# A two-layer diffusion trunk: K and V projected by stream, a hand-given order in the first FFN unit, and the output stored in four parts

## The chip, the cores and the metric

The kernel runs on one core of a Trainium2 chip. The metric is the device time of one launch in microseconds (us), the median of three runs. Five engines work side by side, each with its own instruction queue that it takes strictly in order: PE (TensorE, matrix products; its weight loads are listed as PEld), DVE (VectorE), ACT (ScalarE), POOL (GpSimd) and SP (SyncE, which issues most DMAs). They wait for one another through semaphores. Data come from the chip's main memory by DMA into on-chip memory; PE writes its results into eight accumulator banks (PSUM), of which this kernel gives four to running products (tag `acc`) and four to everything short-lived (tag `aux`).

## The reference, cut to what matters

Two streams of 256 tokens each, the latent `x` (v = 0) and the context `ctx` (v = 1), width D = 1024, go through two layers. Everything is in 32-bit floats.

```
for i in range(2):
    m, mc = split9(silu(c) @ w_ada[i] + b_ada[i]), split9(silu(c_ctx) @ w_ada[i] + b_ada[i])
    x  += 0.5*m[2]  * swiglu(rms(x,  g0)*(1+m[1])  + m[0])          # and xc the same way with mc
    h, hc = rms(x, g1)*(1+m[4]) + m[3], rms(xc, g1)*(1+mc[4]) + mc[3]
    k, v of both streams (two attention branches); q, conv, gates of the latent stream
                                                   (and, in layer 0, of the context as well)
    x  += m[5] * merge(window attention, gated conv, global attention)
    x  += 0.5*m[8] * swiglu(rms(x, g2)*(1+m[7]) + m[6])
return x                                            # latent stream only, (1, 256, 1024)
```

`w_ada[i]` is 1024 x 9216: shift (column block 0) and scale (block 1) of the first norm are needed before the first product of the layer. `swiglu(h) = (silu(h @ wg) * (h @ wu)) @ wd` with an inner width of 2816. The input projection's first 512 columns are K and V of branch a (128 each) and of branch c (128 each).

## The kernel before, in words

**Layout.** Activations are kept transposed, channels on the 128 partitions: `xT` is 128 x 8 x 512 (eight blocks k of 128 channels; columns 0 to 255 are the latent tokens, 256 to 511 the context). Each product is made three times to keep 32-bit accuracy: an operand is split into a high and a low part (`wh`, `wl` for weights; `hh`, `hl` for activations), and PE adds wh·hh, wh·hl and wl·hh (lines 207 to 209, or 1088 to 1090 in the first unit). Splitting 128 x 1024 weights takes a copy on ACT (line 184 or 191) and then a subtraction on DVE (line 185 or 192). The tags `wh` and `wl` have three buffers. One 128-column block of weights against all tokens is 24 products (8 blocks k times 3) into one `acc` bank, 512 columns wide, or 256 wide for one stream alone.

**Order.** The program is written in one thread. A planner then gives each engine its order: an instruction that it thinks ready goes before one that it thinks late, otherwise the earlier-written goes first. On the chip that order is fixed. A small written queue (class `Queue`) lets steps of normalization be written some microseconds "later" between products: `queue.put(lag, tag, step)`, advanced by every product, and `queue.finish(tag)` writes all that is left of a tag.

**Head and first unit** (lines 1016 to 1092). SP issues the loads in this order: identity, x, ctx, and then for kp = 0 to 3 the scale block and the shift block of `w_ada[0]` for channels 256·kp to 256·kp+255 (`ada_load`, line 223, 1 MiB each), with the two halves of the first gate and up weights (512 KiB pieces, line 1010) after kp = 0 and kp = 1. For each stream ACT squares and sums the rows (line 1027), DVE forms the mean (line 379), POOL raises it to -1/2 (line 382), ACT and PE spread it over the partitions (lines 385 and 391), PE transposes the input (line 1034), DVE or ACT copies it into `xT` (1038, 1040), and DVE multiplies it by the spread factor (1046, tiles `xu`). Then for each kp: PE multiplies silu(c), silu(c_ctx) by the two `w_ada` blocks (line 231; 64 columns at a time, one column group for each quarter of the channels), DVE transposes the result and adds bias and gain (238, 240, 248; tiles `mods`), ACT makes `hh` (1075), DVE makes the full value and `hl` (1076, 1079), and PE runs the 24 products of channel blocks 2kp and 2kp+1 into the four banks of `first` (1088 to 1090). The order of these parts on PE is the planner's.

**K and V** (lines 703 to 712, in `mixer`). Each of the two branches b has a 128-column block for K and one for V. `keys(b, v, w)` does one stream at a time, `values(b)` both streams in 512-wide products. Before:

```
            queue.finish(0)
            for b in range(2):
                keys(b, 0, ws[b])
            ws = [split_w(raws[b], KD, slice(0, P)) for b in range(2)]
            queue.finish(1)
            for b in range(2):
                keys(b, 1, ws[b])
            for b in range(2):
                values(b)
```

`queue.finish(1)` writes what is left of the context stream's normalization (lines 418 to 423 and 191/192), which the products of `keys(b, 1)` need. A step after each `keys` makes its own norm: PE sums squares (line 649), DVE, POOL (656) and DVE (658) make the factor, and PE spreads it (line 666). After each `values`, PE turns the result (line 698).

**End.** The last FFN's last `project` runs four column blocks mb of the down projection on the latent stream; each adds into `xT` (line 464). Then 16 transposes (line 1136) fill two 128 x 1024 tiles, copied by DVE (1138) and ACT (1140), each stored by one 512 KiB DMA (1141).

Of the kernel before, what the change touches and what calls it, by code (L numbers as in the profile page):

```python
# [6 lines left out]
F32 = mybir.dt.float32  # L7
# [53 lines left out]
def trunk(ctx, tc, x, c, ctxt, c_ctx, w_ada, b_ada, norm_g, ffn_w_gate, ffn_w_up, ffn_w_down,  # L61
# [157 lines left out]
    def ada_load(pool, i, a, kp):  # L219

        raw = pool.tile([P, KD, WB], F32, tag="adar", name="adar", bufs=6)
        c0 = a * D + kp * WB
        nc.sync.dma_start(out=raw, in_=w_ada[i][:, c0:c0 + WB].rearrange("(k p) f -> p k f", p=P))
        return raw

    def ada_part(raw, i, a, kp):
        ps = aux()
        for k in range(KD):
            r4 = raw[:, k].rearrange("p (m j r) -> p j m r", j=4, r=32)
            for j in range(4):  # L230
                nc.tensor.matmul(
                    ps[32 * j:32 * j + 32, :WB // 4], c32[:, k, :], r4[:, j], start=(k == 0), stop=(k == KD - 1)
                )
        ada_done(i, a, ps, 2 * kp, 2)

    def ada_done(i, a, ps, k0=0, n=KD):
        tt = small.tile([P, S], F32, tag="t1k", name="ada_t", bufs=2)
        nc.vector.transpose(out=tt[:, :32 * n], in_=ps[:, :32 * n])
        m = mods[i][:, KD * a + k0:KD * a + k0 + n, :]
        nc.vector.tensor_tensor(  # L240
            out=m, in0=tt[:, :32 * n].rearrange("p (m r) -> p m r", r=32)[:, :, 0:2],
            in1=b_ada_v(i, KD * a + k0, n).unsqueeze(2).to_broadcast([P, n, 2]), op=ALU.add,
        )
        ada_scale(i, a, m, k0, n)
# [131 lines left out]
    def rstd(sums):  # L376

        var = small.tile([P, 2], F32, tag="var", name="var")
        nc.vector.tensor_scalar(
# [6 lines left out]
        return rr  # L386
# [7 lines left out]
    def norm(v, loose, i, a, h, early=None):  # L394
# [8 lines left out]
        rr = rstd(st[:, 0:2])  # L403
# [35 lines left out]
    def project(streams, tail, nm, chunk, i, a, early=None):  # L439
# [91 lines left out]
    def ffn(i, f, h, streams, side, tail, first=None, early=None):  # L531
        x = parts_of(h)
        with tc.tile_pool(name="ffn", bufs=1) as fp:
# [6 lines left out]
            for f0, fn in ((0, 12), (12, 10)):  # L540
# [54 lines left out]
                h = project(streams, tail if f0 else None, KD // 2, down, i, 6 * f + 2)  # L595
# [4 lines left out]
    def mixer(i, h, streams, tail, early=None):  # L600
# [6 lines left out]
        with tc.tile_pool(name="mix", bufs=1) as mp, tc.tile_pool(name="mixt", bufs=2) as tp:  # L607
# [80 lines left out]
            def values(b):  # L688
                pv = acc()
                mm_chunk(pv, split_w(raws[b], KD, slice(P, 2 * P)), x, 0, KD, KD, slice(0, T))  # L690
                zv = tmp()
                nc.scalar.activation(out=zv, in_=pv, func=AF.Copy)
                queue.put(LAG_SQ, "a", lambda: values_turned(b, zv))

            def values_turned(b, zv):
                tv = aux()
                for t in range(4):
                    nc.tensor.transpose(tv[:, t * P:(t + 1) * P], zv[:, t * P:(t + 1) * P], ident)
                nc.vector.tensor_copy(vt[b].rearrange("p t d -> p (t d)"), tv)
# [7 lines left out]
            ws = [split_w(raws[b], KD, slice(0, P)) for b in range(2)]  # L707
# [307 lines left out]
    for kp in range(KD // 2):  # L1015
        for a in (1, 0):
            adar[kp, a] = ada_load(xin_p, 0, a, kp)
# [4 lines left out]
    junk = xin_p.tile([P, D], F32, name="junk", bufs=1)  # L1022
    un = []
    for v in range(2):
        ss = xin_p.tile([P, 2], F32, tag="ss", name="ss")
        for t in range(2):
            nc.scalar.activation(out=junk, in_=xin[v][:, t, :], func=AF.Square, accum_out=ss[:, t:t + 1])
# [163 lines left out]
```

## Time and profile before

| What | us |
|---|---|
| Median of three runs (2076.76 to 2080.05) | 2077.16 |
| The profiled execution's own time | 2079.74 |
| Span of the profile, first to last instruction | 2077.4 |
| PE busy in the span | 2041.7 (98%) |
| DVE busy, ACT busy, POOL busy | 1403.3, 854.9, 126.0 |
| Mean granted share of PE's clock | 0.997 |

Times below count from the start of the span. A product on PE is listed with its whole duration, but the next one starts before it ends; what one costs in a running stream is the distance between two starts. In the timeline's rows, "[1.85 <-DVE x]" means that the engine had been idle for 1.85 us and DVE's instruction that writes x released it.

### The profile page before, as it was taken

What the parts mean: (1) busy time and instruction counts of PE and PEld (TensorE: products, weight loads), DVE (VectorE), ACT (ScalarE), POOL (GpSimd) and SP (SyncE); (2) the same over time, 40 slices, a digit from 0 to 9 for tenths busy, and PEclk for the clock granted to TensorE, in tenths of its full rate; (3) what the DMA queues carried; (4) which work ended last, traced back from release to release, by engine and by line L of the source; (5) the groups of instructions that cost most, each with busy time, mean ns of one, the idle gap of its engine ahead of it and who ended that gap; (6) DMA issues with size and microseconds to landing.
All of it is one profiled execution on the core that took longest, in us unless ns stands there. A gap on an engine that the chain in (4) does not pass through costs nothing. (4 is left out here: it accounts for less than half of the span.)

```text
span 2077.4 us, 29568 instructions
## 1 busy us (share of the span) xinstructions
PE 2041.7 (98%) x11883; PEld 1755.4 (85%) x11883; DVE 1403.3 (68%) x2174; ACT 854.9 (41%) x1357; POOL 126.0 (6%) x137
## 2 busy tenths in 40 slices
PE   6999999999999999999999999999999999999999
PEld 5888888887777888988888898888889887999998
DVE  4778778667764444677776668778566796667554
ACT  4332222546564233532223254222225577456443
POOL 0000000310000000300000030000003200001000
PEclk9999999999999999999999999999999999999999
DMA  9745554041212333465553327446340432667552
GB/s 316 242 152 193 173 191 139 26 117 54 84 55 68 92 101 118 146 193 162 173 182 123 126 81 229 149 148 220 105 144 26 127 108 87 170 200 231 174 184 73
DMA packets 247765, 295.08 MB, mean 142 GB/s; under 512 B 6708, under 2 KB 228300, under 8 KB 247628
## 3 DMA queue, kind: packets, MB, share of 16 engines
q1 hardware_dynamic: 244812, 288.91, 44.2%
q0 software_dynamic: 2560, 4.20, 1.1%
q8 instruction: 93, 1.52, 0.3%
q14 instruction: 44, 0.36, 0.1%
q10 hardware_dynamic: 256, 0.09, 0.0%
HBM read 287.93 MB, written 1.05 MB: 139 GB/s over the span
## 5 line engine op out<-in xcount | busy, mean ns | idle before, releaser
L207 PE MATMUL acc<-hh,wh 128*128 128x512 f32 (+1 forms) x2208 | 773.3, 351 | 0.8 <-ACT hh L191 0.8
L209 PE MATMUL acc<-hh,wl 128*128 128x512 f32 (+1 forms) x2208 | 769.6, 349 | 2.3 <-DVE wl L185 2.3
L208 PE MATMUL acc<-hl,wh 128*128 128x512 f32 (+1 forms) x2208 | 769.8, 349 | 0.8 <-DVE hl L192 0.8
L184 ACT ACTIVATE wh<-raw 128x1024 fp32r<-128x1024 f32 x328 | 326.2, 997 | 683.2 <-PE acc L208 524.7
L185 DVE TENSOR_TENSOR wl<-raw,wh 128x1024 fp32r<-128x1024 f32 x328 | 375.3, 1146 | 214.2 <-ACT wh L184 211.8
L207 PEld LDWEIGHTS acc<-hh,wh 128*128 128x128 f32 x2208 | 418.9, 190 | 61.1 <-issue 8.6
L209 PEld LDWEIGHTS acc<-hh,wl 128*128 128x128 f32 x2208 | 419.2, 190 | 56.8 <-DVE wl L185 3.1
L208 PEld LDWEIGHTS acc<-hl,wh 128*128 128x128 f32 x2208 | 419.6, 190 | 54.4 <-issue 1.6
L280 DVE SCALAR_TENSOR_TENSOR adac<-adar,c,adac 128x1024 f32<-128x1024 f32 x224 | 280.2, 1282 | 42.8 <-DMA adar<-in_w_ada_dram 42.3
L209 PE MATMUL acc<-gh,wl 128*128 128x512 f32 (+1 forms) x824 | 276.3, 336 | 1.3 <-DVE wl L185 1.3
L207 PE MATMUL acc<-gh,wh 128*128 128x512 f32 (+1 forms) x824 | 277.2, 337 | 0.0
L208 PE MATMUL acc<-gl,wh 128*128 128x512 f32 (+1 forms) x824 | 276.3, 335 | 0.0
L184 ACT ACTIVATE wh<-rawd 128x640 fp32r<-128x640 f32 (+1 forms) x152 | 119.1, 784 | 307.9 <-PE acc L208 296.2
L185 DVE TENSOR_TENSOR wl<-rawd,wh 128x640 fp32r<-128x640 f32 (+1 forms) x152 | 134.8, 889 | 76.3 <-ACT wh L184 76.2
L209 PEld LDWEIGHTS acc<-gh,wl 128*128 128x128 f32 x824 | 156.1, 190 | 18.0 <-DVE wl L185 1.9
L208 PEld LDWEIGHTS acc<-gl,wh 128*128 128x128 f32 x824 | 156.4, 190 | 15.9
L207 PEld LDWEIGHTS acc<-gh,wh 128*128 128x128 f32 x824 | 156.4, 190 | 15.9
L351 POOL TENSOR_TENSOR ssq<-ssq,sq 128x256 f32<-128x256 f32 (+1 forms) x42 | 45.8, 1090 | 1441.7 <-ACT sq L348 1441.7
L575 DVE TENSOR_TENSOR sg<-acc,sg 128x512 f32<-128x512 f32 (+1 forms) x90 | 54.6, 607 | 112.3 <-PE acc L209 108.3
L207 PE MATMUL acc<-slot,wh 128*128 128x256 f32 (+1 forms) x352 | 113.4, 323 | 1.3 <-ACT slot L191 1.3
L209 PE MATMUL acc<-slot,wl 128*128 128x256 f32 (+1 forms) x352 | 113.3, 322 | 0.2 <-DVE wl L185 0.2
L208 PE MATMUL acc<-slot,wh 128*128 128x256 f32 (+1 forms) x352 | 113.2, 322 | 0.0
(185 smaller groups left out, 1858.8 us busy)
## 6 DMA issues: line engine op xcount, KB each, us to landing
adar<-in_w_ada_dram SPq DMA_DIRECT2D x128, 512.0 KB, 3.8
raw<-in_ffn_w_gate_dram SPq DMA_DIRECT2D x43, 1024.0 KB, 9.0
raw<-in_ffn_w_up_dram SPq DMA_DIRECT2D x43, 1024.0 KB, 5.4
rawd<-in_ffn_w_down_dram SPq DMA_DIRECT2D x16, 1536.0 KB, 8.0
raw<-in_w_gate_dram SPq DMA_DIRECT2D x24, 1024.0 KB, 6.6
rawd<-in_ffn_w_down_dram SPq DMA_DIRECT2D x16, 1280.0 KB
raw<-in_w_in_dram SPq DMA_DIRECT2D x16, 1024.0 KB, 5.6
adar<-in_w_ada_dram SPq DMA_DIRECT2D x8, 1024.0 KB, 11.9
```

Of the source, the lines that this page charges most:

```text
L184: nc.scalar.activation(out=wh[:, :kc], in_=raw[:, :kc, cols], func=AF.Copy)
L185: nc.vector.tensor_tensor(out=wl[:, :kc], in0=raw[:, :kc, cols], in1=wh[:, :kc].bitcast(F32), op=ALU.subtract)
L207: nc.tensor.matmul(ps, wh[:, k, :], xh, start=first, stop=False)
L208: nc.tensor.matmul(ps, wh[:, k, :], xl, start=False, stop=False)
L209: nc.tensor.matmul(ps, wl[:, k, :], xh, start=False, stop=last)
L280: nc.vector.scalar_tensor_tensor(out=self.acc[:, v], in0=raw, scalar=c32[:, k, v:v + 1], in1=self.acc[:, v], op0=ALU.mult, op1=ALU.add,)
L351: fold.tensor_tensor(out=ssq[:, ts], in0=ssq[:, ts], in1=sq, op=ALU.add)
L575: nc.vector.tensor_tensor(out=sg[:, ts], in0=ps[1][:, ts], in1=sg[:, ts], op=ALU.mult)
```

## The change

- **Head.** ACT runs a silu on two columns right after its first DMA issues (`warm`); the silu of c comes after the latent stream's two squares. The mean of a stream is written before the copies into `xT`, and for the latent stream DVE's copies are ordered behind it. The multiplication by the spread factor (`normed`) is done for kp = 0 first, for kp = 1 to 3 behind the first modulation.
- **First unit.** The scale and shift blocks of one kp lie side by side in one tile (`adar`, three buffers of 16 KiB a partition instead of six of 8), loaded by four DMAs of 512 KiB instead of two of 1 MiB; PE multiplies 128 columns at once, so there are half as many products, and one transpose on DVE instead of two. `in_turn` fixes PE's order: each part is queued behind the part before it. The order is vectors(0), products k0 (p = gate, then up), vectors(1), k1, k2, vectors(2), k3, k4 gate, vectors(3), k4 up, k5, k6, k7. In each group of six the two weight blocks alternate. `hh`, the full value and `hl` are made channel block by channel block. The second halves of both first weights are split in round kp = 1; one of the four pairs of split halves gets buffers of its own.
- **K and V.** Both are done stream by stream: K then V of the latent stream for both branches, then those of the context in the order K1, V0, K0, V1. K0's weights are split a second time, V's once.
- **End.** After each block mb of the last down projection four transposes and one copy make 256 output columns, stored by a DMA of 256 KiB; for mb = 0 to 2 they are put into the written queue 1.3 us behind the block.

```
-    nc.scalar.activation(
-        out=c32[:, :, 0:2], in_=vb[:, 0:16].rearrange("p (v k) -> p k v", v=2), func=AF.Silu
-    )
+    warm = xin_p.tile([P, 2], F32, tag="ss", name="warm")
+    nc.scalar.activation(out=warm, in_=ones[:, 0:2], func=AF.Silu)
...
-        raw = pool.tile([P, KD, WB], F32, tag="adar", name="adar", bufs=6)
...
+        raw = pool.tile([P, KD, 2, WB], F32, tag="adar", name="adar", bufs=3)
+        for k0 in (0, 4):
+            for a in range(2):
+                nc.sync.dma_start(
+                    out=raw[:, k0:k0 + 4, a], in_=w_ada[i][
+                        k0 * P:(k0 + 4) * P, a * D + kp * WB:a * D + (kp + 1) * WB
+                    ].rearrange("(k p) f -> p k f", p=P)
+                )
...
+            r4 = raw[:, k].rearrange("p a (m j r) -> p j a m r", j=4, r=32)
             for j in range(4):
...
+                m = nc.tensor.matmul(
+                    ps[32 * j:32 * j + 32, :WB // 2], c32[:, k, :], r4[:, j], start=(k == 0), stop=(k == KD - 1)
+                )
...
+    def to_tokens(mb):
+
+        ps = aux()
+        for t in range(2):
+            for e in range(2):
+                c0 = t * WB + e * P
+                nc.tensor.transpose(ps[:, c0:c0 + P], xT[:, 2 * mb + e, t * P:(t + 1) * P], ident)
+        ot = small.tile([P, 2, WB], F32, tag="t2k", name="ot", bufs=4)
+        nc.vector.tensor_copy(ot, ps.rearrange("p (t f) -> p t f", t=2))
+        nc.sync.dma_start(
+            out=out[0][:, mb * WB:(mb + 1) * WB].rearrange("(t p) f -> p t f", p=P), in_=ot
+        )
...
+            if done is not None:
+                if mb == nm - 1:
+                    queue.finish("o")
+                    done(mb)
+                else:
+                    queue.put(LAG_SQ, "o", lambda mb=mb: done(mb))
...
             for b in range(2):
-                keys(b, 0, ws[b])
-            ws = [split_w(raws[b], KD, slice(0, P)) for b in range(2)]
+                keys(b, 0, wk[b])
+            wv = []
+            for b in range(2):
+                wv.append(split_w(raws[b], KD, slice(P, 2 * P)))
+                values(b, 0, wv[b])
             queue.finish(1)
-            for b in range(2):
-                keys(b, 1, ws[b])
-            for b in range(2):
-                values(b)
+            keys(1, 1, wk[1])
+            wk[0] = split_w(raws[0], KD, slice(0, P))
+            values(0, 1, wv[0])
+            keys(0, 1, wk[0])
+            values(1, 1, wv[1])
...
             if v == 0:
-                nc.vector.tensor_copy(to, of)
+                with tc.issue_after(rr[1].ins):
+                    nc.vector.tensor_copy(to, of)
...
+    def in_turn(f, *args):
+        if chain:
+            with tc.issue_after(chain[-1].ins):
+                chain.append(f(*args))
+        else:
+            chain.append(f(*args))
...
+    def first_products(k, p):
+        ws = [[t[:, k % 4, cc * P:(cc + 1) * P] for t in ws0[p, k // 4]] for cc in range(2)]
+        for e, r in ((0, 0), (0, 1), (1, 0)):
+            for cc in range(2):
+                m = nc.tensor.matmul(
+                    first[cc][p], ws[cc][e], h[r][:, k], start=(k + e + r == 0),
+                    stop=(k == KD - 1 and e == 1),
+                )
+        return m
+
+    for p in range(2):
+        split_half(p, 0)
+    in_turn(vectors, 0)
+    end = modulated(0)
+    with tc.issue_after(end.ins):
+        for kp in range(1, KD // 2):
+            for v in range(2):
+                normed(kp, v)
     for kp in range(KD // 2):
...
         if kp == 1:
             load_rest()
...
             for p in range(2):
-                split_half(p, kp // 2)
...
+                split_half(p, 1)
+        in_turn(first_products, 2 * kp, 0)
+        if kp < KD // 2 - 1:
+            if kp < 2:
+                in_turn(first_products, 2 * kp, 1)
+            in_turn(vectors, kp + 1)
+            modulated(kp + 1)
+        if kp >= 2:
+            in_turn(first_products, 2 * kp, 1)
+        for p in range(2):
+            in_turn(first_products, 2 * kp + 1, p)
     make_rest()
```

`vectors(kp)` calls `ada_part(adar[kp], 0, kp)`; `modulated(kp)` holds ACT's and DVE's work of one kp; `issue_after(ins)` orders every instruction of its block behind `ins` on that one's engine, without a wait on another engine.

## Rows read from the trace of the kernel before

**Rows 1.** The page, part 1: busy time of each engine over the span.
```profile
PE 2041.7 (98%) x11883; PEld 1755.4 (85%) x11883; DVE 1403.3 (68%) x2174; ACT 854.9 (41%) x1357; POOL 126.0 (6%) x137
```

**Rows 2.** Waits of PE over the span: total us, times, longest.
```profile
PE acc L1088 <- ACT hh L1075: 6.3, 3, 2.7
PE aux L666 <- DVE slot L658: 4.8, 6, 1.9
```

**Rows 3.** Windows: busy of each engine, granted PE clock, DMA share, GB/s.
```profile
0.00:10.00 10.00, 2.71 (x13) 2.65 (x14) 1.60 (x8) 5.21 (x8) 0.19 (x4) 1.00 0.73 228
10.00:20.00 10.00, 7.92 (x91) 7.30 (x93) 5.86 (x13) 6.27 (x13) 1.37 (x2) 1.00 1.06 348
20.00:40.00 20.00, 14.15 (x293) 10.86 (x282) 12.07 (x28) 6.76 (x11) 0.00 (x0) 0.91 1.09 349
...
26.30:29.70 3.40, 3.40 (x55) 2.86 (x48) 0.86 (x3) 1.06 (x1) 0.00 (x0) 0.50 1.09 348
415.40:418.80 3.40, 3.15 (x14) 3.06 (x15) 2.85 (x9) 2.40 (x5) 2.80 (x3) 0.50 0.00 0
```

**Rows 4.** Timeline of the head: start, duration, engine, line, what.
```profile
7.18 1.28 ACT L134 ACT_TABLE_LOAD   x1
...
13.29 0.79 PE L391 MATMUL aux<-rr,ones 128*128 128x128 f32 x2 [2.08 <-ACT rr L385]
...
18.92 2.22 PE L231 MATMUL aux<-adar,c 128*32 128x64 f32 x128
...
19.54 1.06 ACT L191 ACTIVATE wh<-raw 128x1024 fp32r<-128x1024 f32 x1 [0.78 <-DMA raw<-in_ffn_w_gate_dram]
```

**Rows 5.** Timeline of PE in the first unit.
```profile
43.68 2.66 PE L231 MATMUL aux<-adar,c 128*32 128x64 f32 x176
...
59.99 0.39 PE L1089 MATMUL acc<-hl,wh 128*128 128x512 f32 x1
60.22 0.39 PE L1090 MATMUL acc<-hh,wl 128*128 128x512 f32 x1
```

**Rows 6.** Timeline of ACT and DVE in the first unit.
```profile
19.09 2.48 DVE L1046 TENSOR_TENSOR xu<-xT,aux 128x512 f32<-128x512 f32 x4 [1.85 <-PE aux L391]
21.49 0.37 DVE L238 STREAM_TRANSPOSE ada_t<-aux 128x64 f32<-128x64 f32 x2
...
22.05 1.22 DVE L192 TENSOR_TENSOR wl<-raw,wh 128x1024 fp32r<-128x1024 f32 x1
...
35.22 2.08 ACT L1075 ACTIVATE hh<-xu,mods 128x256 fp32r<-128x256 f32 x4 [5.67 <-DVE mods L240]
35.86 0.91 DVE L1076 TENSOR_SCALAR xu<-xu,mods 128x256 f32<-128x256 f32 x2 [0.67 <-ACT hh L1075]
...
36.80 0.69 DVE L1079 TENSOR_TENSOR hl<-xu,hh 128x512 fp32r<-128x512 f32 x1
```

**Rows 7.** Timeline of K and V in layer 0: POOL, PE and DVE.
```profile
411.07 1.46 DVE L185 TENSOR_TENSOR wl<-raw,wh 128x1024 fp32r<-128x1024 f32 x1
...
411.42 1.97 POOL L656 TENSOR_TENSOR vark<-vark,expo 128x4 f32<-128x4 f32 x1
...
411.65 0.28 PE L209 MATMUL acc<-hh,wl 128*128 128x256 f32 x1
...
413.78 0.71 PE L666 MATMUL aux<-cst,slot 128*128 128x128 f32 x4 [1.85 <-DVE slot L658]
...
420.50 1.22 DVE L185 TENSOR_TENSOR wl<-raw,wh 128x1024 fp32r<-128x1024 f32 x1
```

**Rows 8.** The chain that ended last, near its end: start, us, what.
```profile
2070.51 0.12 PE acc L209
2070.63 1.36 PE aux L1136 x12
```

**Rows 9.** Timeline of the end: DVE and SP.
```profile
2070.66 0.48 DVE L464 SCALAR_TENSOR_TENSOR xT<-acc,mods,xT 128x256 f32<-128x256 f32 x1 [1.31 <-PE acc L209]
...
2073.12 0.36 SPq L1141 DMA_DIRECT2D out_dram<-ot  x1
```

More of the change, by code (lines that the diff above doesn't have):

```diff
@@ new lines, in ada_part @@
+        k0, n = 2 * kp, 2
+        tt = small.tile([P, S], F32, tag="t1k", name="ada_t", bufs=2)[:, :WB // 2]
+        nc.vector.transpose(out=tt, in_=ps[:, :WB // 2])
+        for a in (1, 0):
+            nc.vector.tensor_tensor(
+                out=mods[i][:, KD * a + k0:KD * a + k0 + n, :],
+                in0=tt.rearrange("p (a m r) -> p a m r", a=2, r=32)[:, a, :, 0:2],
+                in1=b_ada_v(i, KD * a + k0, n).unsqueeze(2).to_broadcast([P, n, 2]), op=ALU.add,
+            )
+            ada_scale(i, a, mods[i][:, KD * a + k0:KD * a + k0 + n, :], k0, n)
@@ L437, in gained, with project @@
         )
[L439 removed]
+    def to_tokens(mb):
[9 more added lines that the diff above has]
+        )
+    def project(streams, tail, nm, chunk, i, a, early=None, done=None):
         plan = [(mb, streams) for mb in range(nm)]
@@ L593, in down @@
                     return pm
-                h = project(streams, tail if f0 else None, KD // 2, down, i, 6 * f + 2)
+                h = project(
+                    streams, tail if f0 else None, KD // 2, down, i, 6 * f + 2, None,
+                    to_tokens if f0 and tail is None else None,
+                )
             ada_side.flush(fp, grp)
@@ L1026, in trunk @@
         for t in range(2):
-            nc.scalar.activation(out=junk, in_=xin[v][:, t, :], func=AF.Square, accum_out=ss[:, t:t + 1])
+            sq = nc.scalar.activation(
+                out=junk, in_=xin[v][:, t, :], func=AF.Square, accum_out=ss[:, t:t + 1]
+            )
+        if v == 0:
+            with tc.issue_after(sq.ins):
+                nc.scalar.activation(
+                    out=c32[:, :, 0:2], in_=vb[:, 0:16].rearrange("p (v k) -> p k v", v=2), func=AF.Silu
+                )
+        rr = rstd(ss)
         for kp in range(KD // 2):
@@ L1061, in split_half, with vectors, modulated @@
         split_x(wh, wl, raw0[p][:, 4 * hf:4 * hf + 4])
-        ws0[p] = wh, wl
+        ws0[p, hf] = wh, wl
+    chain = []
+    def in_turn(f, *args):
[4 more added lines that the diff above has]
+            chain.append(f(*args))
+    def vectors(kp):
+        return ada_part(adar[kp], 0, kp)
+    def modulated(kp):
+        for e in range(2):
+            k = 2 * kp + e
+            u = un[kp][:, e]
+            for v in range(2):
+                ts = slice(v * S, (v + 1) * S)
+                scale, shift = (mod_v(0, r, k, v) for r in (1, 0))
+                nc.scalar.activation(out=h[0][:, k, ts], in_=u[:, ts], func=AF.Identity, scale=scale, bias=shift)
+                nc.vector.tensor_scalar(
+                    out=u[:, ts], in0=u[:, ts], scalar1=scale, scalar2=shift, op0=ALU.mult, op1=ALU.add
+                )
+            end = nc.vector.tensor_tensor(out=h[1][:, k], in0=u, in1=h[0][:, k].bitcast(F32), op=ALU.subtract)
+        return end
@@ L1080, in trunk @@
-        if kp % 2 == 0:
-            for p in range(2):
-                split_half(p, kp // 2)
-        for k in (2 * kp, 2 * kp + 1):
-            for cc in range(2):
-                for p in range(2):
-                    wh, wl = (t[:, k % 4, cc * P:(cc + 1) * P] for t in ws0[p])
-                    ps = first[cc][p]
-                    nc.tensor.matmul(ps, wh, h[0][:, k], start=(k == 0), stop=False)
-                    nc.tensor.matmul(ps, wh, h[1][:, k], start=False, stop=False)
-                    nc.tensor.matmul(ps, wl, h[0][:, k], start=False, stop=(k == KD - 1))
+            for p in range(2):
+                split_half(p, 1)
@@ L1126, in trunk @@
         h = ffn(i, 1, h, st, side(4, 34, 2, 2, 1), None if last else (i + 1, 0), early=early)
-    with tc.tile_pool(name="xout", bufs=1) as op:
-        for t in range(2):
-            ot = op.tile([P, D], F32, name=f"ot{t}")
-            for g in range(2):
-                ps = aux()
-                for e in range(4):
-                    k = 4 * g + e
-                    nc.tensor.transpose(ps[:, e * P:(e + 1) * P], xT[:, k, t * P:(t + 1) * P], ident)
-                if t == 0:
-                    nc.vector.tensor_copy(ot[:, g * 512:(g + 1) * 512], ps)
-                else:
-                    nc.scalar.activation(out=ot[:, g * 512:(g + 1) * 512], in_=ps, func=AF.Copy)
-            nc.sync.dma_start(out=out[0, t * P:(t + 1) * P, :], in_=ot)
 def shape_constants():
```

85 lines of the change are left out of this document (31 added, 54 removed).

## The prediction

> **What bounds the kernel now.** I read the page's busy times first. PE is busy for 98% of the span [rows 1]; every other engine has slack, so PE's own work counts in full and anything else counts only where PE waits for it. Next the waits of PE over the whole span: the largest that the change can touch are ACT's `hh` in the first unit (6.3 us in 3 waits) and the K norm's factor, line 666 (4.8 us in 6, three a layer) [rows 2]. Third, windows: from 10 to 40 us the DMA engines are full, at 348 and 349 GB/s, and in three short stretches PE runs at half its clock [rows 3]; two are shown, and layer 1 repeats that of K and V. Then timelines of the head, the first unit, K and V, and the end. PE stops three times before 60 us because the `w_ada` products of one kp stand behind the products of the kp before: 18.92 for the first, 43.68 for a group that holds two [rows 4, 5]. The first unit's last product starts at 60.22 [rows 5].
>
> **The floor of the first unit is the DMA.** Up to the last `w_ada` block SP asks for 0.07 MB of identity, 2.1 MB of x and ctx, 8.4 MB of `w_ada` and 2.1 MB of first weights, 12.7 MB. The windows moved 2.3 MB by 10 us and 3.5 by 20 [rows 3]; the other 6.9 MB at 349 GB/s take 19.8 us, so the last block lands at about 40, the one before at 34, the second at 25. The change loads the same bytes in the same order. After 40 the new order leaves: vectors(3); 18 products (k4 up, k5); 24 products (k6, k7). A product costs 0.23 (60.22 less 59.99) [rows 5]. vectors(3) is 64 passes of 128 columns where before two parts had 128 of 64. At 43.68 176 passes took 2.66, 15.1 ns each [rows 5]; if a pass costs by its columns vectors(3) takes 128 x 15.1 = 1.9, if by the count half of that, 1.0. Neither row tells which; I take 1.9, since columns do set the cost of products (0.23 for 512, 0.12 for 256 [rows 5, 8]). So the earliest end is 40 + 1.9 + 4.1 + 5.5 = 51.5, against 60.45 now: 8.9 us to be had at most.
>
> **First unit: what I take.** Can the others keep up? From 20.6, when the first half weights are split on ACT (19.54 + 1.06 [rows 4]), DVE has four subtractions of weights at 1.22, six `normed` at 0.62, and per kp two instructions of the `mods` kind pair (transpose to last bias, 0.56 from 21.49 to 22.05, a little more as one chain; I say 1.0), four line-1076 steps at 0.41 and two `hl` at 0.69 [rows 6], where 0.41 is 0.91 for two less the stop between them: 4.9 + 3.7 + 4 x 4.0 = 24.6 us. Run without a gap that ends at 45.2; PE wants the last `hl` at 40 + 1.9 + 4.1 + 2.7 = 48.7. It fits with 3.5 us to spare, but DVE waits for ACT's `hh` (0.5 each [rows 6]) and for DMA, and a `hl` that comes late stops all of PE's fixed order behind it. If the two late weight subtractions stand before the second round's vectors on DVE, that round comes 2.4 us later and half a round of products with it. I allow 2.1 us: end at 53.6, **6.8 us gained**. Ends: 8.9 (nothing late) and 3.0 (every round late by its `hh`, two `hl` and a bias chain that PE can't cover, 3 rounds x 2 us). The half clock of 26.3 to 29.7 lies in both versions' idle part before the weights are there; a repeat costs 1.7, which is within the allowance.
>
> **Head.** A table load of 1.28 leaves ACT, the mean no longer waits for four copies, and the spread at 13.29, which had kept PE idle for 2.08 [rows 4], comes some 2 us earlier. This moves vectors(0) from 18.92 to about 16.5, but the first product needs `wh` at 20.6, and vectors(1) the block of 25. I count nothing for it: the loads cover it. Without that cover it would be worth 2.
>
> **A rule that speaks against the split loads.** From 10 to 40 us 1 MiB blocks and 512 KiB weight pieces share the queue, at 348 and 349 GB/s [rows 3]. The Trainium skill, DMA: Bandwidth & Descriptors, Rules for kernel authors, asks for 1 MiB or more per DMA for full bandwidth; sixteen 512 KiB loads in place of eight of 1 MiB would by that rule land late, and with nothing left of the first unit's 6.8 the sum would be 4.5 instead of 11.3; the trace does not bear it out, as several loads are in flight at once. As a mechanism of this kernel: at the 228 GB/s of the first ten microseconds [rows 3], 8.4 MB take 12.7 us longer.
>
> **K and V, per layer.** *Removed:* PE stands from 411.77 to 413.78, 2.0, before line 666, because POOL's power (1.97 us) and DVE's copy are not done and the context's `hh`, `hl` aren't there either [rows 7]; then 3.4 us at half clock, in which 1.7 are lost [rows 3]. *Added:* V in 96 products of 256 columns in place of 48 of 512: 96 x 0.12 - 48 x 0.227 = 0.63 [rows 5, 8]. Four evacuations and four turns in place of two are narrower, same columns, hidden under PE. One split less: nothing on the path. *Moved:* K's context products now come behind 5.8 us of V's latent products, which need only `h` of the latent stream and V's split. That split is the third and fourth in the ring of three buffers, where the fourth was done at 411.07 + 1.46 = 412.5 [rows 7], in time for the second V block at about 415. What stays: line 666 is placed where the planner thinks the factor ready, and the chip's power takes longer; with products to run meanwhile, PE still arrives early by half or so. I take 1.0 of the 2.0 back, and the clock's 1.7: 1.0 + 1.7 - 0.63 = 2.1 a layer, **4.1 for two**. Upper end: all of it, 3.1 a layer, 6.2. Lower end: no wait shortened and the clock still down, -0.63 a layer, -1.3. Queued behind a late line 666 is all of PE.
>
> **End.** *Before:* the last product starts at 2070.51, the second 512 KiB store is issued at 2073.12 and the span ends at 2077.4, 4.3 later [rows 8, 9]. *After:* twelve of sixteen transposes, 0.113 each (1.36 for 12 [rows 8]), go between earlier products: +1.36 on PE, same work as before but no longer at the end. Behind the last product: `xT` 2070.66 + 0.48 = 2071.14, three transposes and their latency 0.6, a copy of 128 x 512, 0.69 [rows 9, 6], so the store is issued at 2072.45, 0.67 earlier. It carries 256 KiB instead of 512 KiB behind another 512: at 349 GB/s 0.75 us of data against 1.5, and nothing ahead of it, so I take 1.1 less. -0.67 - 1.1 + 1.36 = **-0.4**; from -1.2 (nothing of the earlier store was in the way less) to +0.7 (no shorter landing).
>
> **Sum.** 6.8 + 4.1 + 0.4 = 11.3. The profiled execution took 2079.74 (span 2077.4 and 2.3 around it), so 2068.4 is forecast for it; the median of the runs shown is 2077.16, 2.6 lower, and 11.3 off that is 2065.9. I say **2066**. A measurement of this kernel can tell about 0.2%, 4.2 us, from no change.
>
> **Rivals.**
> - *DVE sets the pace of the first unit.* For: 24.6 us of work in 28; a fixed order on PE. Against: the work fits. Gain there 3.0, in all 7.5: 2069.7. 15%.
> - *A new wait takes the place of the one at line 666.* V's subtraction is queued on DVE behind the context's normalization, as the one at 420.50 was, whose own weights were ready long before [rows 7], and PE stops for it at 415. Against: the third and fourth split came early. K and V then give 0: 2070.0. 15%.
> - *The half-sized loads land late.* 12.7 us by the rate above: 2077.2 - 11.3 + 12.7 = 2078.6, no change that can be told. For: the start of the trace. Against: both full windows. 3%.
> - *No gain:* the loads hide the order, the gaps of PE move and don't shrink, K and V as in the second rival: about 2074.5. 5%.
> - *Slower: PE stays at half clock in the first unit.* After idle stretches the clock was down for 3.4 us [rows 3]. If the new order makes PE pause in every round and the clock stays down through it, a product costs 0.46 and 96 of them 22 us more. It decides from 67 products at half clock on (11.3 + 4.2 = 15.5, by 0.23 each); with all 96, 2088. For: PE waits for DMA in each round. Against: before, it paused three times in 30 us and the clock was down once. 2%.
>
> **Numbers.** Forecast 60%: 2066, its own range 2062 to 2069.5. Low end: all upper ends together are 8.9 + 6.2 + 1.2 = 16.3, 2060.9; I take 2061.5. High end: the first two rivals are inside at 2070, and both together at 2073.9 are left out with the rest; 2072.5. Faster by over 0.2% (below 2073): forecast and the first two rivals, 0.90; within: half-sized loads and no gain, 0.08; slower: 0.02.
>
> **What the profile after would show.** Line 231's successors in one run of 64 per kp, about 1.9 us each, the last near 40 to 42; the first unit's last product at 52 to 55 instead of 60.2; PE's waits for `hh` down from 6.3 to under 2. In K and V no pause near 2 us and a granted clock of 1.00 there. A store of 256 KiB issued some 2 us after the last product. I am wrong if the loads up to 40 us fall below 340 GB/s, if PE's waits for DVE's `hl` or `wl` grow by more than 5 us, or if K and V show half clock again.

## The result, and the profile after

The changed kernel took 2067.9 us in the median of four runs (2066.91 to 2070.31), the kernel before on the same chip 2077.6 (2076.76 to 2080.05). The ratio is 0.9949, 95% interval 0.9937 to 0.9961, some 10.6 us less by the ratio and 9.7 by the medians; 2066 was forecast. The profiled execution took 2066.98, with a span of 2065.2: 12.2 shorter than the profiled one of before. Line numbers below are those of the changed kernel: its 1141 is 1088 to 1090 before, 1130 is 1075, 1134 is 1079, 235 is 231 and 692 is 666.

The page of the changed kernel, span and busy times, against [rows 1]:

```profile
span 2065.2 us, 29245 instructions
...
PE 2039.0 (99%) x11723; PEld 1757.4 (85%) x11723; DVE 1401.2 (68%) x2174; ACT 850.3 (41%) x1357; POOL 123.8 (6%) x137
```

PE is busy 2.7 us less, in a span shorter by 12.2: most of the gain is waiting that is gone. Waits of PE over the span, against [rows 2]:

```profile
PE acc L1141 <- ACT hh L1130: 2.5, 1, 2.5
PE aux L692 <- DVE slot L684: 1.9, 4, 0.7
PE acc L206 <- ACT slot L190: 1.7, 1, 1.7
```

The three waits for `hh` in the first unit are one, before its first product. The K factor has kept 1.9 of 4.8. The third wait lies outside the change, and before it was 1.3. Timeline of PE in the first unit, against [rows 4, 5]:

```profile
14.93 1.08 PE L235 MATMUL aux<-adar,c 128*32 128x128 f32 x32
16.55 1.08 PE L235 MATMUL aux<-adar,c 128*32 128x128 f32 x32 [0.54 <-DMA adar<-in_w_ada_dram]
20.15 1.11 PE L1141 MATMUL acc<-hh,wh 128*128 128x512 f32 x2 [2.51 <-ACT hh L1130]
21.80 1.22 PE L1141 MATMUL acc<-hl,wh 128*128 128x512 f32 x2 [0.54 <-DVE hl L1134]
...
26.36 2.30 PE L235 MATMUL aux<-adar,c 128*32 128x128 f32 x64
...
32.22 0.73 PE L1141 MATMUL acc<-hl,wh 128*128 128x512 f32 x2 [0.17 <-DVE hl L1134]
...
34.73 1.95 PE L235 MATMUL aux<-adar,c 128*32 128x128 f32 x64
...
40.95 1.96 PE L235 MATMUL aux<-adar,c 128*32 128x128 f32 x64
...
52.23 0.63 PE L1141 MATMUL acc<-hh,wl 128*128 128x512 f32 x2
```

From 20.15 on PE stops twice, for `hl`, at 21.80 and 32.22, and then runs without a gap to the last product at 52.47. Windows, against [rows 3]: busy times of PE, PEld, DVE, ACT and POOL, the granted clock, the DMA share and GB/s.

```profile
10.00:20.00 10.00, 5.98 (x94) 4.76 (x92) 5.01 (x13) 6.74 (x15) 0.93 (x2) 1.00 1.07 373
20.00:40.00 20.00, 19.14 (x179) 14.29 (x180) 15.73 (x34) 8.19 (x14) 0.00 (x0) 0.83 1.08 374
20.29:27.12 6.83, 6.29 (x28) 4.11 (x32) 6.76 (x13) 1.73 (x3) 0.00 (x0) 0.50 1.09 379
...
395.06:450.86 55.80, 54.12 (x355) 48.86 (x353) 35.31 (x73) 28.14 (x52) 14.42 (x16) 1.00 0.38 105
859.97:866.80 6.83, 6.83 (x34) 6.83 (x34) 3.67 (x5) 3.31 (x5) 1.62 (x1) 0.50 1.09 357
1846.42:1849.84 3.42, 3.42 (x19) 3.42 (x18) 2.34 (x4) 2.16 (x4) 0.00 (x0) 0.50 0.04 8
```

Three things stand here. The loads run faster from 10 to 40 us, at 373 and 374 GB/s in place of 348 and 349. The half clock (0.50, which is 1.2 GHz of 2.4) lies on the first unit's products now, for 6.83 us; K and V have none left. And two stretches that the change doesn't touch run at half clock: at 860 for 6.83 us, where before it was 3.41 at 872.8 (the prediction counted three stretches before, and this is a fourth), and at 1846, where before there was none.

**The ledger.** To see where a kernel gains or loses, its span is cut at starts on PE: the first unit's last product; the last product ahead of K and V in a layer; the first sum of that layer's queries. The first two lines are times from the start of the span, the others lengths. "Old head" to "together" are experiments, below. From the first unit's last product to layer 0's K it is 342.6 us in all eight.

| us | before | after | old head | 1 MiB | free order | idle filled | later factor | together |
|---|---|---|---|---|---|---|---|---|
| first product | 23.81 | 20.15 | 21.64 | 23.12 | 20.67 | 21.21 | 21.02 | 20.91 |
| last product of first unit | 60.22 | 52.47 | 54.09 | 56.58 | 55.12 | 52.39 | 52.91 | 52.06 |
| K and V, layer 0 | 59.27 | 55.80 | 55.79 | 55.77 | 55.76 | 55.78 | 54.34 | 54.33 |
| on to layer 1's K | 1143.29 | 1144.84 | 1143.63 | 1142.31 | 1144.90 | 1142.29 | 1143.39 | 1142.06 |
| K and V, layer 1 | 48.37 | 45.15 | 45.14 | 45.14 | 45.12 | 45.13 | 43.76 | 43.74 |
| rest of the span | 423.67 | 424.35 | 420.88 | 421.02 | 420.91 | 420.84 | 422.22 | 422.43 |

Before to after: 7.75 in the first unit, 3.47 and 3.22 in K and V, 1.55 lost between the layers and 0.68 in the rest: 12.2.

### The profile page after: what moved, and what is told of

Read it like the earlier page. It is cut to its first block, busy times and chain, and to the rows that moved or that the text cites. A ratio compares the mean times of both kernels' runs of the same rounds, so it can differ in the third digit from the quotient of the medians.

```text
span 2065.2 us, 29245 instructions
## 1 busy us (share of the span) xinstructions
PE 2039.0 (99%) x11723; PEld 1757.4 (85%) x11723; DVE 1401.2 (68%) x2174; ACT 850.3 (41%) x1357; POOL 123.8 (6%) x137
## 4 chain that ended last, share of the span: by engine, by line
PE 92%; DVE 3%; ACT 2%; POOL 1%; DMA 1%; issue 1%; SPq 0%; ACTq 0%; POOLq 0%; DVEq 0%
PE acc L206 28%; PE acc L208 28%; PE acc L207 28%; PE aux L896 2%; PE aux L884 2%; PE acc L1141 1%; PE aux L838 1%; PE aux L841 1%; POOL u L427 1%; DVE wl L184 1%; ACT wh L183 1%; ACT hh L190 0%; DMA raw<-in_ffn_w_gate_dram 0%; DVE u L422 0%; PE aux L404 0%
## 5 line engine op out<-in xcount | busy, mean ns | idle before, releaser
L183 ACT ACTIVATE wh<-raw 128x1024 fp32r<-128x1024 f32 (+1 forms) x326 | 323.7, 996 | 682.8 <-PE acc L207 521.3
L184 DVE TENSOR_TENSOR wl<-raw,wh 128x1024 fp32r<-128x1024 f32 (+1 forms) x326 | 371.8, 1143 | 217.5 <-ACT wh L183 215.5
L206 PEld LDWEIGHTS acc<-hh,wh 128*128 128x128 f32 x2240 | 425.2, 190 | 60.5 <-issue 8.6
L208 PEld LDWEIGHTS acc<-hh,wl 128*128 128x128 f32 x2240 | 425.1, 190 | 55.0 <-DVE wl L184 2.8
L207 PEld LDWEIGHTS acc<-hl,wh 128*128 128x128 f32 x2240 | 425.4, 190 | 52.6 <-issue 1.7
```

The lines of the kernel that those rows point to most:

```text
L183: nc.scalar.activation(out=wh[:, :kc], in_=raw[:, :kc, cols], func=AF.Copy)
L184: nc.vector.tensor_tensor(out=wl[:, :kc], in0=raw[:, :kc, cols], in1=wh[:, :kc].bitcast(F32), op=ALU.subtract)
L206: nc.tensor.matmul(ps, wh[:, k, :], xh, start=first, stop=False)
L207: nc.tensor.matmul(ps, wh[:, k, :], xl, start=False, stop=False)
L208: nc.tensor.matmul(ps, wl[:, k, :], xh, start=False, stop=last)
```

## The experiments

The experiments ran in three groups, each on a chip of its own: the first four of the table, those from "1 MiB loads" to "idle filled", and the rest. Beside them the kernel before had medians of 2077.72, 2079.73 and 2078.94, so across groups the ratios compare and the medians only roughly. Each kernel was profiled once.

| kernel | median, us | ratio to before [95%] | span profiled |
|---|---|---|---|
| first unit and head alone | 2069.71 | 0.9963 [0.9949, 0.9976] | 2069.7 |
| K and V alone | 2073.38 | 0.9974 [0.9965, 0.9983] | 2071.0 |
| end alone | 2077.04 | 0.9999 [0.9990, 1.0008] | 2074.5 |
| old head | 2064.32 | 0.9935 [0.9923, 0.9948] | 2062.1 |
| 1 MiB loads | 2065.21 | 0.9935 [0.9922, 0.9949] | 2063.4 |
| half the loads | 2064.34 | 0.9931 [0.9919, 0.9943] | 2063.2 |
| free order | 2063.04 | 0.9932 [0.9920, 0.9945] | 2064.4 |
| idle filled | 2061.58 | 0.9919 [0.9905, 0.9932] | 2059.0 |
| later factor | 2061.03 | 0.9919 [0.9905, 0.9934] | 2059.2 |
| sum first | 2063.14 | 0.9927 [0.9914, 0.9940] | 2059.6 |
| together | 2061.64 | 0.9922 [0.9908, 0.9936] | 2057.2 |
| normed later | 2061.34 | 0.9917 [0.9903, 0.9931] | 2060.3 |

**The three parts alone.** The kernel before, with one part each.

> Only the head and the first unit are changed; K, V and the end are those of before. If the parts simply add, the first unit's last product starts near 52.5 as with the whole change, and the time is 7.8 us under before (ratio 0.9963), two thirds of the whole gain. Rival: what the first unit gains is partly lost again later (a colder clock or a wait that moves), and the time is under 5 us better (ratio over 0.9976) although the first unit ends at 52.5.

> Only K and V by stream; head, first unit and end are those of before. From the two profiles, the stretch from the first K product to the sums of the queries is 3.5 us shorter in layer 0 and about the same in layer 1: 6.7 us in all, ratio 0.9968, with no stretch at half clock near 415 and 1617. My prediction said 4.1 (0.9980): 1.0 of each 2.0 us wait back, the clock's 1.7 back, 0.63 paid. Rival: the gain is only that of the clock, which may fall elsewhere; then the waits before the K factor are as long as before and the time is within 2 us of before.

> Only the output in four parts; all else is before. The prediction gives 0.4 us, from 1.2 better to 0.7 worse, ratio 0.9994 to 1.0003, and a last store issued some 2 us after the last product that lands in about 2 us. Rival: the four stores with rows of 1 KiB or the twelve transposes between products cost more than the shorter end gives, and the time is 1 us or more worse.

Measured: 0.37%, 0.26% and 0.01%. They add to 0.64%, 13 us, and the whole gave 0.51%: within the intervals they add, with perhaps a little lost. With K and V alone the two stretches of K and V are 55.79 and 45.13 us long, as with the whole change, and no half clock lies in them: the ledger's 3.5 and 3.2 are the change's own. The interval of its ratio holds both figures that were expected, 0.9968 and 0.9980. The end's worth can't be told from nothing by its time. In the ledger the rest of the span is 420.8 to 421.1 with the new end wherever PE hardly waits near 1850 and the K factor stands as it did, and 421.4 to 421.5 with the old one (before, and the two parts that keep the old end, less those waits): 0.6 by the middle values, 420.9 and 421.45. With the first unit alone its first product came at 21.39 and its last at 53.84, 1.4 behind the whole change, from the same code: single executions of one first unit differ by that much.

**Old head.**

```
-    warm = xin_p.tile([P, 2], F32, tag="ss", name="warm")
-    nc.scalar.activation(out=warm, in_=ones[:, 0:2], func=AF.Silu)
...
-                with tc.issue_after(rr[1].ins):
-                    nc.vector.tensor_copy(to, of)
+                nc.vector.tensor_copy(to, of)
```

(silu of c back to where it was, and the mean back behind the copies; the new order of `normed` stays)

> The whole change, but with the head of before: no early table load for the silu, the silu of c where it stood, a stream's mean behind the copies into xT. My prediction counts nothing for the head, since the loads cover it: then the first unit ends within 0.5 us of 52.7 and the time is that of the whole change (10.6 us under before). Rival: PE's fixed order has no slack after its first product, so a head that is 2 to 3 us later moves the end of the first unit by 2 to 3 us, and the time is 7 to 9 us under before.

2064.32, a ratio of 0.9935 against 0.9949 for the whole change, whose intervals overlap: no slower than with the new head, against both expectations. The ledger tells why the time says little of the head: in the first unit the old head is 1.6 us behind the changed kernel, and it keeps that until 859; it then wins 1.2 between the layers, where its half clock lasts 3.41 in place of 6.83, and 3.5 in the rest, where it has neither the wait at 1843 nor the half clock behind it. Of the 1.6, four executions with the new head and the same first unit (first products 20.15, 21.39, 21.02, 21.69, mean 21.06; last products 53.06 in the mean) leave 0.6 for the head by the first product and 1.0 by the last, and they spread over 1.5 themselves. What the start follows is a load. ACT's first two steps for the first product, in the changed kernel and then with the old head:

```profile
18.05 1.06 ACT L190 ACTIVATE wh<-raw 128x1024 fp32r<-128x1024 f32 x1 [2.84 <-DMA raw<-in_ffn_w_gate_dram]
...
19.02 1.08 ACT L1130 ACTIVATE hh<-xu,mods 128x256 fp32r<-128x256 f32 x2
```

```profile
19.54 1.06 ACT L191 ACTIVATE wh<-raw 128x1024 fp32r<-128x1024 f32 x1 [2.83 <-DMA raw<-in_ffn_w_gate_dram]
20.51 1.08 ACT L1125 ACTIVATE hh<-xu,mods 128x256 fp32r<-128x256 f32 x2
```

PE's wait is put down to `hh`, but `hh` stands behind ACT's copy of the first weights, and ACT had been idle for 2.8 us until these weights landed. The first product starts 2.10 behind the copy's start in both. In all five executions, this one and the four above, it is 2.09 or 2.10, and only the landing moves, from 18.05 to 19.60.

What the head does bring is a faster load from 20 us on, by the same window of two kernels, first the old head's, then that of the first unit and head alone:

```profile
20.00:40.00 20.00, 17.37 (x172) 13.05 (x173) 15.06 (x31) 8.47 (x14) 0.00 (x0) 0.83 1.09 349
```

```profile
20.00:40.00 20.00, 17.68 (x173) 13.27 (x174) 15.25 (x31) 8.49 (x15) 0.00 (x0) 0.83 1.09 381
```

The loads are the same sixteen in both. From 20 to 36 us the four kernels with the old head moved 348 or 349 GB/s, and those with the new one and all its loads 381 to 383. PE's time from first to last product is 32.45 in both: there it doesn't notice.

**1 MiB loads.**

```
-        for k0 in (0, 4):
-            for a in range(2):
-                nc.sync.dma_start(out=raw[:, k0:k0 + 4, a], in_=w_ada[i][
...
+        for a in (1, 0):
+            c0 = a * D + kp * WB
+            nc.sync.dma_start(out=raw[:, :, a], in_=w_ada[i][:, c0:c0 + WB].rearrange("(k p) f -> p k f", p=P))
```

> The whole change, but each kp's scale block and shift block come in one load of 1 MiB each, as before, into the pair tile. If the size of a load does not matter to what the queue moves: windows of 10 to 20 and 20 to 40 us within 2% of those of the changed kernel (373 and 374 GB/s), the first product of the first unit within 0.5 us of 20.15 and its last within 0.5 us of 52.5, time 2067.9 give or take 2. By the rule for larger loads (the Trainium skill, DMA: Bandwidth & Descriptors, Rules for kernel authors) the windows would rise, with the time unchanged where PE is the bound. If it is the alternation of four pieces that raised the rate from 349, the windows fall back to 349 GB/s and the last w_ada block lands 2 us later, near 40.4.

Windows of this kernel, and its PE at the start of the first unit:

```profile
10.00:20.00 10.00, 7.62 (x98) 6.90 (x96) 4.13 (x9) 5.39 (x13) 0.73 (x2) 1.00 1.05 358
20.00:40.00 20.00, 15.19 (x144) 11.06 (x148) 14.54 (x30) 7.74 (x12) 0.00 (x0) 0.83 1.09 384
```

```profile
17.97 1.95 PE L233 MATMUL aux<-adar,c 128*32 128x128 f32 x64 [1.90 <-DMA adar<-in_w_ada_dram]
23.12 0.76 PE L1139 MATMUL acc<-hh,wh 128*128 128x512 f32 x2 [3.19 <-ACT hh L1128]
```

From 20 to 36 us both move 383 GB/s: neither size nor alternation makes the rate. The first unit, expected unmoved, ends 4.1 us later: the passes can't begin on half a block and start at 17.97, not 14.93, of which 0.8 is a later first load, and the first product comes 3.0 later (2.1 behind the mean of 21.06). The other 1.1 lies behind the first product, and its cause stays open. The Trainium skill, DMA: Bandwidth & Descriptors, Rules for kernel authors, wants 1 MiB or more per DMA for full bandwidth; no loss with halves shows in these traces (383 GB/s with either), and the gain of halves is that they are ready earlier.

**Half the loads.**

```
-        for k0 in (0, 4):
+        for k0 in (0,):
...
-            r4 = raw[:, k].rearrange("p a (m j r) -> p j a m r", j=4, r=32)
+            r4 = raw[:, k % 4].rearrange("p a (m j r) -> p j a m r", j=4, r=32)
```

> The whole change with the second half of every w_ada[0] scale and shift block left out (4.2 of 8.4 MB before the first unit ends): the products take the first half twice. If the loads are the floor of the first unit, its last product comes some 8 us earlier than 52.5, since its last block lands near 27 instead of 38.5. If PE is the floor from its first product on, the 32.3 us from first product (20.15) to last (52.5) stay within 1 us, and only the start can move: by at most the 2.8 us that one MiB takes at 375 GB/s, for the first half weights come that much earlier. Time then 2065 to 2068.

This kernel leaves out the second half of every block. With 4.2 MB less to load the first unit's last product came at 55.13, later than 52.47, and first to last took 32.96 in place of 32.32. So from the first product on the loads are no floor. The start, expected earlier by up to 2.8, was 2.0 later, and another wait had taken the load's place there. Its DVE and PE:

```profile
18.06 1.23 DVE L191 TENSOR_TENSOR wl<-raw,wh 128x1024 fp32r<-128x1024 f32 x1 [1.04 <-ACT wh L190]
...
19.20 0.31 DVE L240 STREAM_TRANSPOSE ada_t<-aux 128x128 f32<-128x128 f32 x1
...
19.70 1.22 DVE L191 TENSOR_TENSOR wl<-raw,wh 128x1024 fp32r<-128x1024 f32 x1
20.83 0.15 DVE L252 SCALAR_TENSOR_TENSOR mods<-mods,vl 128x4 f32<-128x4 f32 x1
...
22.17 1.22 PE L1141 MATMUL acc<-hh,wh 128*128 128x512 f32 x2 [4.05 <-ACT hh L1130]
```

DVE's order has changed with the loads: one subtraction of weights stands ahead of the vectors' transpose and one ahead of the last step of `mods`, and `hh` waits for that step.

**Free order.**

```
-        if chain:
-            with tc.issue_after(chain[-1].ins):
-                chain.append(f(*args))
-        else:
-            chain.append(f(*args))
+        chain.append(f(*args))
```

> The whole change without the written order of the first unit: PE's order there is the planner's. If the order is what gains in the first unit, its last product comes between 56 and 60 us instead of 52.5 and the time is 2071 to 2075. Rival: the halved count of w_ada passes and the block-by-block hh and hl do it, the planner's order is as good: last product within 1 us of 52.5, 2068.

55.12, between the two: 34.45 from first to last product against 32.32. By this pair of executions the written order is worth 2.1 (2.5 against the mean of the four above, 32.0); the other 5.1 of the 7.75 come without it, 3.1 of them in an earlier first product. The time of 2063.04 doesn't show the loss, which the rest of its span pays back with 3.4 (no wait at 1843). Its five runs are 2062.76 to 2063.04 and 2066.17 and 2067.33; the profiled one, with 6.83 us at half clock at 862, is the 2066.17.

**Idle filled.**

```
+    def idle_products():
+        ps = aux()
+        for _ in range(12):
+            m = nc.tensor.matmul(ps[:, :P], ones, ident, start=True, stop=True)
+        return m
+    in_turn(idle_products)
```

> The whole change with twelve products more, of ones with the identity, which nothing reads, behind vectors(0), where PE stands idle from 17.4 to 20.15. If the half clock from 20.3 to 27.1 follows from that idle stretch, it is gone or shorter: the last product of the first unit comes up to 3.4 us earlier, near 49, unless hh or hl becomes what PE waits for. Rival: the clock falls all the same, as twelve products of 128 columns are little work; no change, 52.5. The time is 2064.5 by the first and 2068 by the second, give or take 2 for the stretches at 860 and 1846 us.

The same window of its profile, and then DVE, ACT and PE around vectors(1):

```profile
20.29:27.12 6.83, 6.04 (x87) 4.68 (x85) 6.76 (x12) 2.65 (x5) 0.00 (x0) 1.00 1.09 380
```

```profile
28.67 0.31 DVE L240 STREAM_TRANSPOSE ada_t<-aux 128x128 f32<-128x128 f32 x1
...
29.29 1.23 DVE L191 TENSOR_TENSOR wl<-raw,wh 128x1024 fp32r<-128x1024 f32 x1
29.41 2.08 ACT L1130 ACTIVATE hh<-xu,mods 128x256 fp32r<-128x256 f32 x4 [1.18 <-DVE mods L252]
...
30.56 0.73 PE L1141 MATMUL acc<-hh,wh 128*128 128x512 f32 x2 [0.41 <-ACT hh L1130]
...
32.14 0.72 PE L1141 MATMUL acc<-hl,wh 128*128 128x512 f32 x2 [0.85 <-DVE hl L1134]
```

The half clock is gone, and with it little: the last product at 52.39 against 52.47 (31.18 from the first against 32.32), where up to 3.4 were to be had. Over the executions it is more, but still under 1: 53.06 in the mean of the four above, 52.20 in the mean of the three kernels that fill this stretch (one of them with `normed` moved as well, below). DVE has no idle time ahead of its transpose at 28.67, and PE stands for `hh` and `hl` until 32.14, where in the changed kernel it came late by itself and had 0.17 to wait at 32.22. Two bounds lay on one another. This execution had no half clock up to the end of PE's work, and took 2060.8.

**Later factor.**

```
-                queue.put(LAG_RSTD, "k", lambda: keys_normed(b, v))
+                queue.put(3.3, "k", lambda: keys_normed(b, v))
```

> The whole change with one number: the step that spreads the K factor (line 692) is written 3.3 us of products behind its squares instead of 2.0. If PE only arrives too early there, its waits at that line (1.0 and 0.67 in layer 0, 0.98 and 0.5 in layer 1) go, and the stretch of K and V up to the queries' sums (line 785) is 1.6 shorter in layer 0 and 1.4 in layer 1; the time is 3 less than the changed kernel's, 2065, if the stretches at 860 and 1846 us stay as they are. Rival: the accumulator banks that the later step holds, or the split behind the last K, become the wait in its place: no gain, 2068.

K and V took 54.34 and 43.76, 1.46 and 1.39 less, as the first of the two expectations had it; no wait at the spread is left. In layer 1 it is given back at once, most of it (about 1.0) because the queries now wait for their own transfer; the rest of the span grows by 1.4:

```profile
1648.24 0.47 PE L838 MATMUL aux<-kk,qs 128*128 128x512 f32 x1 [0.87 <-DMA qs<-qs]
```

2061.03 is the lowest median of all, but its ratio of 0.9919 stands level with that of "idle filled". Of the 6.0 us between its span and the changed kernel's K and V have 2.85, the way between the layers 1.45 and the rest 2.1, less 0.44 in the first unit.

**Sum first.** Layer 1, the second block of `w_o`; `sums` holds line 1004's instructions.

```
+                    if i == 1 and mb == 1:
+                        with tc.issue_after(sums[-1].ins):
+                            w = split_w(raws[mb], KD, slice(e * P, (e + 1) * P))
```

> The whole change with one edge in layer 1: the weight subtraction of the second w_o block, which in the changed kernel stood on DVE ahead of the merge's last sum (line 1004) and waited for a load with it, is queued behind that sum. If that order made PE's wait at 1843.45 to 1845.47, the wait is under 0.5 us; and if the half clock from 1846.4 to 1849.8 followed from it, it is gone too: 1.5 and 1.6 us less, 2065. Rival: the load itself is what PE needs next, so that the wait only moves to the second block: 2068.

What it is about, in the changed kernel:

```profile
1842.32 1.06 ACT L183 ACTIVATE wh<-raw 128x1024 fp32r<-128x1024 f32 x1 [1.76 <-DMA raw<-in_w_o_dram]
...
1843.40 1.23 DVE L184 TENSOR_TENSOR wl<-raw,wh 128x1024 fp32r<-128x1024 f32 x1 [1.64 <-ACT wh L183]
...
1844.55 0.42 DVE L1004 TENSOR_TENSOR slot<-slot,tmp 128x256 f32<-128x256 f32 x1
1845.00 0.42 ACT L190 ACTIVATE slot<-slot 128x256 fp32r<-128x256 f32 x1 [1.63 <-DVE slot L1004]
...
1845.47 0.50 PE L206 MATMUL acc<-slot,wh 128*128 128x256 f32 x2 [1.74 <-ACT slot L190]
```

A load that lands late holds ACT's copy, this DVE's subtraction, and that the sum queued behind it, which PE needs. With the edge there was no such wait and no half clock there: 2063.14. It decides nothing, since eight executions without the edge hardly have the wait either (under 0.6 from start to start), while the kernel before has it (1.5 at 1857) and K and V alone too (2.7 at 1849), neither with half clock behind it. What makes the load late stays open.

**Together, and normed later.** The three edits in one; then the `normed` of kp = 2 and 3 queued behind the next rounds' `hl` as well.

> The changed kernel with the three edits in one: the twelve idle products behind vectors(0), the K factor 3.3 us behind, the merge's last sum ahead of the second w_o block's subtraction. If they add: 2061.6 measured with the idle products alone, less 3 for the factor, and nothing more for the sum where that wait is already short: 2058.5, below both kernels. Rival: the half clock comes back somewhere else, 3.4 us at a time for 1.7 lost: 2060 to 2062.

> The one before with the six normed of the first unit parted: those of kp = 2 and 3 are queued behind the next rounds' hl instead of all six behind the first. With PE at full clock DVE was without a gap from 20.1 to 29, and PE waited 0.4 and 0.85 us for hh and hl at 30.6 and 32.1. If DVE's chain set the pace there, those waits go and the first unit's last product comes 1.0 to 1.3 us earlier than in the kernel before; the time is 1 less, 2057.5. Rival: the loads or PE set it: no change.

The terms add in the profile: 52.06, 54.33, 43.74, no half clock up to the end, 2058.98. But its five runs reach 2063.88, with a median of 2061.64, no lower than the idle products or the later factor alone. All three lie below the kernel before and the changed kernel; which is best can't be told. With `normed` parted, DVE waits for PE, and PE for the load:

```profile
26.62 1.08 PE L235 MATMUL aux<-adar,c 128*32 128x128 f32 x32 [0.68 <-DMA adar<-in_w_ada_dram]
```

```profile
27.76 0.32 DVE L240 STREAM_TRANSPOSE ada_t<-aux 128x128 f32<-128x128 f32 x1 [1.74 <-PE aux L235]
```

The last product is at 52.15, 0.1 later: behind half clock and DVE's chain stood the second block of vectors, all three within about 1 us.

## Why the prediction was right, and where its steps failed

The forecast of 11.3 met 12.2 in the profile and about 10.6 by the ratio of the runs. Against the ledger: first unit +0.95, K and V +2.6, end +0.2, and 2.8 lost in places that the sum didn't have. The two mechanisms, PE's order in the first unit and K and V by stream, gained where the prediction said; that the total came so near is in part luck, for its own terms came to 15.0 and the losses elsewhere brought that back.

- **The floor of the first unit was the wrong one.** It was put on the DMA, at 40 for the last block. The rate rose, that block landed at 38.5, and with half of it left out nothing came earlier. What holds from the first product on is PE: 96 products at 0.23, three vectors parts at 1.9, 3.4 lost to the clock and the stops for `hl` make 32. That 53.6 was forecast and 52.70 came is luck in this term: a sum of the right size on another ground. Over the executions it fits even better: 60.0 in the mean of three with the old first unit, 53.1 of four with the new: 6.9, forecast 6.8.
- **128 columns.** The choice of 1.9 for 64 passes was right: 1.95 and 1.96; 2.30 where the clock was half for a part of it.
- **DVE's pace** was allowed 2.1 and is one of two equal bounds at 32; the rival in which every round is late didn't come, for vectors(2) and vectors(3) find their work done.
- **The head at nothing.** The size holds within the scatter (0.6 to 1.0), and so does its ground: the loads cover it. The first product's wait of 2.51 is named for `hh`, but `hh` stands behind the copy of the first weights, which began when their load landed at 18.05, and at 19.54 with the old head. The spread came at 10.77 in place of 13.29 and the passes at 14.93 (16.5 was forecast), and PE then stood still for 2.5 all the same.
- **The half clock "within the allowance".** It lay on the products and took twice as long as assumed; that it cost under 1 us ("idle filled") is DVE's doing.
- **K and V, mis-sized: 2.1 a layer, measured 3.5 and 3.2.** Clock and added products were right: 1.7 gained, and 0.8 by the ledger's remainder for the 0.63. But I took back 1.0 of one stop of 2.0, while PE stood for 4.0 in layer 0: [rows 2] counts six waits for the factor, and the stops of about 0.5 (two more for the factor, one for `hl`, one for the turned values) have gone too, but for one. Left are 0.9 and 0.55, and the later factor took just these.
- **The end**: 0.4 forecast, 0.6 in the ledger, nothing that a time could show. The store of 256 KiB was issued at 2062.20, 2.2 behind the last product, as forecast.
- **One sign missed.** PE's waits for `hh` were to fall from 6.3 to under 2, and 2.5 stayed, all of it ahead of the first product. The other signs came, but that the first passes run as two groups of 32, as the two halves of their block land.
- **What the sum didn't have.** Between the layers 3.41 us more at half clock cost 1.5; in layer 1 the late `w_o` load and the half clock behind it take about 1.3 more than before. Across 14 profiled executions that stretch at 860 shows none, 3.41 or 6.83 us of half clock (six, five and three times), and the way to layer 1's K is 1142.1 to 1142.3, 1143.3 to 1143.7 and 1144.8 to 1145.0. Together with a wait near 1850 this is some 6 us between kernels that do the same there. Why all four runs of the changed kernel lie above the medians of its variants stays open: one of them is profiled, and the two stretches explain that one (2066.98 less 2.6 and 3.5 is 2060.9).

## What to carry to other kernels

Compare two variants by a ledger of starts on the bound engine before their times are compared: here half clock and a wait far from the edit moved the times by some 6 us, and "free order", which lost 2 us in the edited stretch, came out with the lower time. A stop has a queue of successors: at 32 us half clock, DVE's chain and a load lay within 1 us, so taking away one bought under 1 of the 3.4 hoped for. The wait that a trace names may itself stand behind another: here `hh` stood behind a copy, and the copy behind a load. In counting what a reorder gives back, count each of the waits that a row lists, not the longest alone.

## What the runs showed of the hardware

- The same loads from one queue moved 348 or 349 GB/s with the old head and 381 to 383 with the new one, from 20 to 36 us, in four and nine kernels; packets of 1 KiB took 51 and 46 ns in the median. Loads of 1 MiB and of 512 KiB stand on both sides, so neither their size nor their alternation makes it; which of the head's edits does, and how, is not shown.
- Up to the last product PE's granted clock fell to 0.50 in pieces of 3.41 or 6.83 us. In the first unit it fell within PE's idle stretch ahead of the first product, or up to 0.6 us behind it, in the eight kernels with the new first unit that leave that stretch idle, and in the three that fill it with twelve products it stayed away. At 860 it came or stayed away after one and the same stop of 1.0 to 1.2 us, in the changed kernel this one, where it came:

```profile
859.42 0.38 PE L404 MATMUL aux<-ones,ssq 128*128 128x1 f32 x2 [0.68 <-POOL ssq L355]
```
